# Linear attention of layer 0 in 64-wide blocks, with the small matmuls of a job issued back to back

## The chip, the cores and the metric

One core of one Trainium2 chip runs the whole program. The metric is the device time in microseconds (us) of one execution; the profile is one further execution, recorded by the hardware profiler.

## The reference, cut to what matters

The program is a two-layer trunk (512 tokens, width 1024). Layer 0 mixes tokens with two kinds of linear attention, layer 1 with softmax attention; both have an MLP and a gated side input. The change concerns the second kind of layer 0, with 8 heads of 64 columns:

```python
def rwkv7_scan(r, decay, k, v, kk, a):          # state: [B, H, 64, 64]
    def step(state, inp):
        r_t, w_t, k_t, v_t, kk_t, a_t = inp
        sa = jnp.einsum('bhvk,bhk->bhv', state, -kk_t)
        state = (state * w_t[:, :, None, :] + sa[..., None] * (kk_t * a_t)[:, :, None, :]
                 + v_t[..., None] * k_t[:, :, None, :])
        return state, jnp.einsum('bhvk,bhk->bhv', state, r_t)
```

The kernel does it in chunks of 64 tokens: inside a chunk the recurrence becomes products of 64x64 matrices and one triangular inverse, and a 64x64 state per head goes from chunk to chunk.

## The kernel before, in words

Tiles have 128 partitions, so two heads of 64 columns lie on top of each other: hp = 0 to 3 is a pair of heads, h = 0, 1 the head in it. The 512 tokens are 8 chunks, and g = 0, 1 is a half of four chunks: a = 0, 1 counts pairs of chunks and c_ = 0, 1 the chunk in the pair. One (hp, g) is called a unit here; there are 8 of them. Every matmul of a unit writes a PSUM tile of the ring "pmr", which has four buffers.

- `pre(hp)` makes the vectors of a head pair: bh, kh, the two rows of ar, v.
- `p1(hp, g)` copies bh and kh into BH, a tile in which each head has its own half of the columns and zeros in the other half (L596, ScalarE). The scores come from 8 matmuls of 128 rows and 128 columns (L600); 8 masked products on VectorE (L605) put 64x64 blocks into NA and KA, zeros elsewhere. Eight transposes (L614) are copied to TOK and, with zeros around, to BZ (L617, L619). Four matmuls with KA give TOK's third part (L625), four more the first part of y (L631, copied at L632).
- `p2(hp, g)` inverts four triangular matrices in fp16 (L664 to L684; its first copy is L640) and applies the inverse in four matmuls (L690); the result is MU (L693).
- `p3(hp, g)` makes for each a the state transitions GB and the inputs HS (matmuls L707, L710, L711; L714 on VectorE, L718 on ScalarE), then steps the state (L744, L746), and in `inner` corrects rh_ and y with four matmuls each (L726 and L727, L731 and L732). L754 reads the states.
- `tail(hp)` normalizes and gates the output.

`hgrn` is the other kind of attention (its own PSUM ring "pmh"), the projections are matmuls of 512 columns in three passes (`mm3`, L244 to L246), and `out_piece` adds both results, projected, to x.

Order: every traced instruction has a rank, its place in the program. A scheduler lays out each engine's queue ahead of time: of the instructions that are ready in its own simulation the lowest rank goes first. `tc.high_priority(offset=n)` lowers the ranks inside it by n; `run` does so by 300 for p1, p2, p3 and tail, which `weave` interleaves. On the chip each engine takes its queue strictly in that order. The steps of a head pair follow the string ORDER: A (p2 of half 0 with the p3 of the pair before and p1 of half 1), F (projections), H (hgrn), B, O (out_piece of the pair before), C (p2 of half 1 with the next pre and p3 of half 0, then the next p1).

Of the kernel before, what the change touches and what calls it, by code (L numbers as in the profile page):

```python
# [12 lines left out]
F32 = mybir.dt.float32  # L13
# [21 lines left out]
OFS = 300  # L35
NWARM = 9
# [149 lines left out]
def trunk(ctx, tc, wts, xT, pT, vecs, lora, cst, lev, seg, rope, gain, out, upto="all", dbg=None, mode=None):  # L186
# [97 lines left out]
    class Stats:  # L284
# [4 lines left out]
        def add(self, sq, rhs):  # L289
            for j in range(NJ):  # L290
# [35 lines left out]
    def bcast_rows(rt, cols, pool, tag):  # L326
# [5 lines left out]
        for j in range(NJ):  # L332
# [31 lines left out]
    def layer0_mixer(actp):  # L364
        ph = ExitStack()
        mp = ph.enter_context(tc.tile_pool(name="mp", bufs=1))
        BH = mp.tile([P, 2, 4, P], F32, name="BH")
        NAs = [mp.tile([P, 2, 2, 2, P], F32, name=f"NA{i}") for i in range(2)]
        KAs = mp.tile([P, 2, 2, 2, P], F32, name="KA")
        BZ = [mp.tile([P, 2, 2, 2, P], F32, name=f"BZ{i}") for i in range(2)]  # L370
# [3 lines left out]
        early = [BH, KAs, *NAs, *BZ, GB, SB, PP]  # L374
# [141 lines left out]
        def four(lhs, rhs):  # L516
            ps = pmr.tile([P, S], F32, name="pmr")
            for i in range(4):
# [7 lines left out]
        def pre(hp, r, k, v):  # L526
# [38 lines left out]
            V.tensor_mul(kk, kk, ps)  # L565
            yield
# [9 lines left out]
            V.tensor_mul(bh, bh, pi)  # L576
# [5 lines left out]
            V.tensor_mul(kh, kh, pi)  # L582
            pre_[hp] = (lw, bh, kh, ar, rh_, bo, dl, v, E("y", 2))
# [3 lines left out]

        def p1(hp, g):
            lw, bh, kh, ar, rh_, bo, dl, v, y = pre_[hp]
            gs = slice(g * 256, g * 256 + 256)  # L590
            NA, KA, TOK = NAs[g], KAs, []
            un[hp, g] = (NA, TOK)

            for n, (src, dst) in enumerate(((bh, NA), (kh, KA))):
                for h in range(2):
                    A.copy(BH[hs[h], n, :, hs[h]], src[hs[h], gs].rearrange("p (c t) -> p c t", t=64))  # L596
                ps = pmr.tile([P, S], F32, name="pmr")
                for c_ in range(4):
                    o = g * 256 + c_ * 64
                    T.matmul(ps[:, c_ * P:c_ * P + P].rearrange("p (x t) -> p x t", x=2), BH[:, n, c_, :],  # L600
                             ar[:, :, o:o + 64], start=True, stop=True)
                pv = ps.rearrange("p (a c x t) -> p a c x t", a=2, c=2, x=2)
                for h in range(2):
                    for c_ in range(2):
                        V.tensor_tensor(dst[hs[c_], :, h, :, hs[c_]], pv[hs[h], :, c_, :, :],  # L605
                                        tri[hs[h], None, :, :].to_broadcast([64, 2, 2, 64]), op=OP.mult)
                yield
            for a in range(2):
# [4 lines left out]
                for n, src in enumerate((ar[:, 0, :], v, bh, kh)):  # L613
                    T.transpose(ps[:, n * P:n * P + P], src[:, js], ident)  # L614
# [9 lines left out]
            for i, (a, h) in enumerate(pk):  # L624
                T.matmul(ps[:, i * 64:i * 64 + 64], KA[:, a, h, 0, :], TOK[a][:, 1, hs[h]], start=True, stop=True)  # L625
            for a in range(2):
                A.copy(TOK[a][:, 2, :], ps[:, a * P:a * P + P])
            yield
            ps = pmr.tile([P, S], F32, name="pmr")
            for i, (a, h) in enumerate(pk):  # L630
                T.matmul(ps[hs[h], a * P:a * P + P], TOK[a][:, 1, hs[h]], KA[:, a, h, 1, :], start=True, stop=True)  # L631
            A.copy(y[:, gs], ps[:, :256])  # L632
            yield

        def p2(hp, g):
# [3 lines left out]
            for a in range(2):  # L639
                A.copy(n16[:, 2 * a:2 * a + 2, :], NA[:, a, :, 0, :])  # L640
# [6 lines left out]
            for l in range(1, 6):  # L647
# [12 lines left out]
                def half4(lhs, rhs):  # L660
                    ps = pmr.tile([P, S], F32, name="pmr")
                    pv = ps[:, :256].rearrange("p (i n u) -> p i n u", i=4, u=H)
                    for i in range(4):
# [11 lines left out]
            for i, (a, h) in enumerate(pk):  # L675
                T.matmul(ps[:, i * P:i * P + P], NA[:, a, h, 0, :], tt[:, i, :], start=True, stop=False)
# [5 lines left out]
            for i in range(4):  # L682
# [6 lines left out]
            for i, (a, h) in enumerate(pk):  # L689
                T.matmul(ps[:, i * P:i * P + P].rearrange("p (x f) -> p x f", x=2), tt[:, i, :],  # L690
                         TOK[a][:, 0::2, hs[h]], start=True, stop=True)
            MU = E("MU", 2, [P, 2, 2, P])
            A.copy(MU.rearrange("p a x (h f) -> p a h x f", h=2),  # L693
                   ps.rearrange("p (a h x f) -> p a h x f", a=2, h=2, x=2))
            un[hp, g] = (NA, TOK, MU)
            yield

        def p3(hp, g):
            lw, bh, kh, ar, rh_, bo, dl, v, y = pre_[hp]
            NA, TOK, MU = un.pop((hp, g))  # L700
# [3 lines left out]
            for a in range(2):  # L704
                bz = BZ[g][:, a]
                ps = pmr.tile([P, S], F32, name="pmr")
# [640 lines left out]
```

## Time and profile before

| | us |
|---|---|
| median of 3 runs | 1511.24 (1509.82 to 1512.02) |
| the profiled execution, its own time | 1511.89 |
| its span, first to last instruction | 1510.1 |
| TensorE / VectorE / ScalarE / GpSimd busy | 1478.1 / 937.6 / 663.1 / 138.4 |
| mean granted TensorE clock, share of full speed | 0.997 |

Busy time of TensorE contains the modelled end of each matmul, so a busy engine is not one at its peak. A plain fp32 matmul is recorded as two instructions, an fp32r or fp16 one as a single one.

### The profile page before, as it was taken

How to read it: one execution, taken by the hardware profiler on the slowest of the kernel's cores; microseconds unless marked ns; L12 is line 12 of the kernel's file. 1: busy time of each engine (PE TensorE's matmuls, PEld its weight loads, DVE VectorE, ACT ScalarE, POOL GpSimd, SP SyncE). 2: the span in 40 equal slices, each digit the busy share in tenths (PEclk: the TensorE clock that was granted, in tenths of full speed). 3: DMA queues.
4: the chain of work that ended last, by engine and by line, in shares of the span. 5: the costliest groups of instructions: out<-in, count | busy, mean ns of one | idle time of the engine just before them, and what ended most of it. 6: DMA issues, size and time to landing. Idle time of an engine off the chain costs nothing.

```text
span 1510.1 us, 20495 instructions
## 1 busy us (share of the span) xinstructions
PE 1478.1 (98%) x7546; PEld 1191.3 (79%) x7546; DVE 937.6 (62%) x1835; ACT 663.1 (44%) x1269; POOL 138.4 (9%) x133
## 2 busy tenths in 40 slices
PE   8899999999989999999999999999999999999998
PEld 6678777777667888888888888777778888888887
DVE  6878797687785664444446648377575444445463
ACT  4675545554446433333334534455634333333342
POOL 4121220310205000000000200000220000000000
PEclk9999999999999999999999999999999999999999
DMA  5110111211123233333333432221123333333331
GB/s 179 56 36 22 55 50 39 66 29 47 39 91 106 90 98 98 98 98 98 98 95 98 124 118 84 77 63 50 56 80 95 95 101 98 98 96 93 98 98 70
DMA packets 67109, 123.88 MB, mean 82 GB/s; under 512 B 7632, under 2 KB 8016, under 8 KB 67008
## 3 DMA queue, kind: packets, MB, share of 16 engines
q1 hardware_dynamic: 65376, 118.57, 25.6%
q10 hardware_dynamic: 1152, 2.43, 0.5%
q0 software_dynamic: 480, 1.57, 0.3%
q8 instruction: 59, 0.97, 0.3%
q14 instruction: 42, 0.34, 0.1%
HBM read 120.45 MB, written 2.10 MB: 81 GB/s over the span
## 4 chain that ended last, share of the span: by engine, by line
PE 87%; DVE 7%; ACT 3%; issue 2%; DMA 1%; POOL 1%; SPq 0%; DVEq 0%; ACTq 0%; POOLq 0%
PE pj L244 20%; PE pj L246 20%; PE pj L245 20%; PE pmr L1273 1%; PE pmr L245 1%; PE pmr L1249 1%; PE pmr L246 1%; PE pmr L244 1%; PE pj L1176 1%; PE pmr L1176 1%; PE pj L1178 1%; PE pmr L1177 1%; PE pmr L1178 1%; PE pj L1177 1%; PE pmh L1176 1%
## 5 line engine op out<-in xcount | busy, mean ns | idle before, releaser
L236 ACT CAST whi<-wr 128x512 fp32r<-128x512 f32 x428 | 265.0, 621 | 549.2 <-PE pj L245 421.9
L237 DVE TENSOR_TENSOR wlo<-wr,whi 128x512 fp32r<-128x512 f32 x428 | 312.5, 733 | 197.6 <-ACT whi L236 193.6
L244 PE MATMUL pj<-act,whi 128*128 128x512 f32 (+1 forms) x856 | 338.1, 396 | 1.2 <-DVE h L935 1.0
L245 PE MATMUL pj<-act,whi 128*128 128x512 f32 (+1 forms) x856 | 336.8, 394 | 0.0
L246 PE MATMUL pj<-act,wlo 128*128 128x512 f32 (+1 forms) x856 | 335.7, 393 | 0.5 <-DVE wlo L237 0.5
L244 PE MATMUL pj<-hid,whi 128*128 128x512 f32 x512 | 199.2, 389 | 0.0
L245 PE MATMUL pj<-hid,whi 128*128 128x512 f32 x512 | 199.2, 389 | 0.0
L246 PE MATMUL pj<-hid,wlo 128*128 128x512 f32 x512 | 199.2, 389 | 0.0
L244 PEld LDWEIGHTS pj<-act,whi 128*128 128x128 f32 x856 | 161.1, 188 | 34.4 <-ACT k L491 1.4
L246 PEld LDWEIGHTS pj<-act,wlo 128*128 128x128 f32 x856 | 161.2, 188 | 32.5 <-DVE wlo L237 1.5
L245 PEld LDWEIGHTS pj<-act,whi 128*128 128x128 f32 x856 | 161.2, 188 | 31.1 <-issue 1.5
L1115 DVE TENSOR_TENSOR x<-x,pj 128x512 f32<-128x512 f32 x128 | 88.0, 688 | 80.6 <-PE pj L246 80.2
L245 PEld LDWEIGHTS pj<-hid,whi 128*128 128x128 f32 x512 | 96.1, 188 | 20.0
L244 PEld LDWEIGHTS pj<-hid,whi 128*128 128x128 f32 x512 | 96.1, 188 | 19.9
L246 PEld LDWEIGHTS pj<-hid,wlo 128*128 128x128 f32 x512 | 96.1, 188 | 19.9
L319 POOL TENSOR_TENSOR acc<-acc,xsq 128x512 f32<-128x512 f32 x35 | 48.7, 1393 | 628.8 <-ACT xsq L313 616.0
L1104 DVE SCALAR_TENSOR_TENSOR r<-pj,rb 128x512 f32<-128x512 f32 x56 | 38.7, 691 | 84.0 <-PE pj L246 84.0
L278 DVE TENSOR_TENSOR hid<-r,hid 128x512 fp32r<-128x512 f32 x64 | 44.3, 691 | 41.5 <-ACT hid L277 41.4
L1105 ACT ACTIVATE r<-r 128x512 f32<-128x512 f32 x64 | 40.5, 632 | 21.6 <-DVE r L1104 21.5
L277 ACT CAST hid<-r 128x512 fp32r<-128x512 f32 x64 | 39.8, 621 | 1.9
L280 ACT ACTIVATE act<-x,vec 128x512 fp32r<-128x512 f32 x32 | 22.9, 720 | 29.4 <-DVE x L1133 12.7
L244 PE MATMUL pj<-os,whi 128*128 128x512 f32 x64 | 28.3, 445 | 4.4 <-DVE x L946 2.8
(387 smaller groups left out, 2225.8 us busy)
## 6 DMA issues: line engine op xcount, KB each, us to landing
wr<-in_wts_dram SPq DMA_DIRECT2D x428, 256.0 KB, 2.7
x<-in_xT_dram SPq DMA_DIRECT2D x8, 256.0 KB, 6.3
sr<-in_wts_dram SPq DMA_DIRECT2D x8, 256.0 KB, 5.3
out_dram<-x SPq DMA_DIRECT2D x7, 256.0 KB, 2.0
r<-in_pT_dram ACTq DMA_DIRECT2D x4, 256.0 KB, 3.0
lw<-in_lora_dram POOLq DMA_DIRECT2D x4, 192.0 KB, 3.1
tq<-in_rope_dram ACTq DMA_DIRECT2D x1, 512.0 KB, 6.7
tk<-in_rope_dram ACTq DMA_DIRECT2D x1, 512.0 KB, 7.6
```

Source lines behind the costliest of these rows:

```text
L236: A.copy(hi, raw)
L237: V.tensor_sub(lo, raw, hi.bitcast(F32))
L244: T.matmul(ps, wh, xh, start=first, stop=False)
L245: T.matmul(ps, wh, xl, start=False, stop=False)
L246: T.matmul(ps, wl, xh, start=False, stop=last)
L277: A.copy(h, src)
L278: V.tensor_sub(l, src, h.bitcast(F32))
L319: G.tensor_add(self.t, self.t, sq)
L1104: V.scalar_tensor_tensor(r, q, 0.0, nf[0], op0=OP.max, op1=OP.mult)
L1105: A.activation(r, r, AF.Square)
L1115: V.tensor_add(x[k], x[k], ps)
L1176: T.matmul(ps[j], xh, wh, start=k == 0, stop=False)
```

## The change

The products work on single 64x64 blocks. `bk` holds bh and kh chunk by chunk in one tile, without BH. The scores come from 16 matmuls with 64 rows, 64 stationary columns and 128 moving columns, which take the four quarters of TensorE's array in turn. For the second kind of key the chunk's block lands on the other half of the partitions, so v is copied once per head pair with the two chunks of a pair swapped (`vx`), KA shrinks to the swapped blocks, and the y part that L631 made is gone: it falls out of `inner`, whose stationary operand W now spans both kinds. `p3` makes all transitions and inputs in one job of 16 matmuls with 64 stationary and 64 moving columns, and `inner` is one such job of 16. HS moves from ScalarE to one product on VectorE, and y's addition becomes a copy on ScalarE. `together` and `tight` lower the rank of all matmuls of a job but the first by 40 more; `tight` is put around all loops of small matmuls of layer 0, those of hgrn and the helpers included (`four`, `half4`, `Stats.add`, `bcast_rows`).

```diff
+TIGHT = 40
+    def tight(jobs):
+        for i, job in enumerate(jobs):
+            with tc.high_priority(offset=TIGHT) if i else ExitStack():
+                yield job
...
-        BH = mp.tile([P, 2, 4, P], F32, name="BH")
-        NAs = [mp.tile([P, 2, 2, 2, P], F32, name=f"NA{i}") for i in range(2)]
-        KAs = mp.tile([P, 2, 2, 2, P], F32, name="KA")
-        BZ = [mp.tile([P, 2, 2, 2, P], F32, name=f"BZ{i}") for i in range(2)]
+        NAs = [mp.tile([P, 2, 2, P], F32, name=f"NA{i}") for i in range(2)]
+        KAs = mp.tile([P, 2, 2, P], F32, name="KA")
+        RRs = [mp.tile([P, 2, 2, 2, 64], F32, name=f"RR{i}") for i in range(2)]
+        BKs = [mp.tile([P, 2, 2, P], F32, name=f"BK{i}") for i in range(2)]
+        Ws = [mp.tile([P, 2, 2, 2, P], F32, name=f"W{i}") for i in range(2)]
...
+            vx = E("vx", 1)
+            for c_ in range(2):
+                A.copy(vx.rearrange("p (j c t) -> p j c t", c=2, t=64)[:, :, 1 - c_],
+                       v.rearrange("p (j c t) -> p j c t", c=2, t=64)[:, :, c_])
...
-            V.tensor_mul(bh, bh, pi)
+            V.tensor_mul(bk[:, :, 0::3, :], jc(bh), jc(pi))
...
-            V.tensor_mul(kh, kh, pi)
+            V.tensor_mul(bk[:, :, 1:3, :], jc(kh), jc(pi))
...
+        def together(jobs):
+            for i, (out, lhs, rhs) in enumerate(jobs):
+                with tc.high_priority(offset=TIGHT) if i else ExitStack():
+                    T.matmul(out, lhs, rhs, start=True, stop=True)
...
-            for n, (src, dst) in enumerate(((bh, NA), (kh, KA))):
-                for h in range(2):
-                    A.copy(BH[hs[h], n, :, hs[h]], src[hs[h], gs].rearrange("p (c t) -> p c t", t=64))
-                ps = pmr.tile([P, S], F32, name="pmr")
-                for c_ in range(4):
-                    o = g * 256 + c_ * 64
-                    T.matmul(ps[:, c_ * P:c_ * P + P].rearrange("p (x t) -> p x t", x=2), BH[:, n, c_, :],
-                             ar[:, :, o:o + 64], start=True, stop=True)
-                pv = ps.rearrange("p (a c x t) -> p a c x t", a=2, c=2, x=2)
-                for h in range(2):
-                    for c_ in range(2):
-                        V.tensor_tensor(dst[hs[c_], :, h, :, hs[c_]], pv[hs[h], :, c_, :, :],
-                                        tri[hs[h], None, :, :].to_broadcast([64, 2, 2, 64]), op=OP.mult)
-                yield
+            pq = [pmr.tile([P, S], F32, name="pmr").rearrange("p (c a x t) -> p c a x t", c=2, a=2, x=2)
+                  for h in range(2)]
+            for a in tight(range(2)):
+                for c_ in range(2):
+                    o = g * 256 + a * P + c_ * 64
+                    for n in range(2):
+                        at = bk[:, 2 * g + a, 3 * c_ if n == 0 else 1 + c_, :]
+                        for h in range(2):
+                            T.matmul(pq[h][hs[c_ ^ n], c_, a], at[hs[h]], ar[hs[h], :, o:o + 64],
+                                     start=True, stop=True)
+            yield
+            for h in range(2):
+                for r in range(2):
+                    V.tensor_tensor(NA[hs[r], :, h, hs[r]], pq[h][hs[r], r, :, 0, :],
+                                    tri[hs[r], 0:1, :].to_broadcast([64, 2, 64]), op=OP.mult)
+                V.tensor_tensor(RR[:, :, h].rearrange("p a c t -> p c a t"), pq[h][:, :, :, 1, :],
+                                tri[:, 1:2, None, :].to_broadcast([P, 2, 2, 64]), op=OP.mult)
+                for r in range(2):
+                    V.tensor_tensor(KA[hs[r], :, h, hs[1 - r]], pq[h][hs[r], 1 - r, :, 0, :],
+                                    tri[hs[r], 0:1, :].to_broadcast([64, 2, 64]), op=OP.mult)
+            yield
...
+                A.copy(BKs[g][:, a], pv[:, 2:4, :])
                 for c_ in range(2):
-                    A.copy(BZ[g][hs[c_], a, :, c_, :], pv[hs[c_], 2:4, :])
+                    A.copy(W_[hs[1 - c_], a, c_, 1, :], pv[hs[1 - c_], 1, :])
...
-            for i, (a, h) in enumerate(pk):
-                T.matmul(ps[hs[h], a * P:a * P + P], TOK[a][:, 1, hs[h]], KA[:, a, h, 1, :], start=True, stop=True)
-            A.copy(y[:, gs], ps[:, :256])
...
-            for a in range(2):
-                A.copy(n16[:, 2 * a:2 * a + 2, :], NA[:, a, :, 0, :])
+            A.copy(n16, NA.rearrange("p a h t -> p (a h) t"))
...
-            A.copy(MU.rearrange("p a x (h f) -> p a h x f", h=2),
-                   ps.rearrange("p (a h x f) -> p a h x f", a=2, h=2, x=2))
+            for c_ in range(2):
+                A.copy(Ws[g][hs[c_], :, c_].rearrange("p a x (h f) -> p a h x f", h=2), pv[hs[c_]])
...
-            for a in range(2):
-                bz = BZ[g][:, a]
-                ps = pmr.tile([P, S], F32, name="pmr")
-                T.matmul(ps[:, :256], MU[:, a, 0, :], bz[:, 0].rearrange("p c f -> p (c f)"), start=True, stop=True)
-                for c_ in range(2):
-                    o = ps[:, 256 + c_ * P:256 + c_ * P + P]
-                    T.matmul(o, bz[:, 0, c_, :], MU[:, a, 1, :], start=True, stop=False)
-                    T.matmul(o, bz[:, 1, c_, :], TOK[a][:, 1, :], start=False, stop=True)
...
+            for k in range(4):
+                a, c_ = divmod(k, 2)
+                w, b = W_[:, a, c_], BKs[g][:, a, c_]
+                jobs += [(pv[hs[h], k, 0], w[:, 0, hs[h]], b[:, hs[h]]) for h in range(2)]
+                jobs += [(pv[hs[h], k, 1], b[:, hs[h]], w[:, 1, hs[h]]) for h in range(2)]
+            together(jobs)
+            yield
+            for h in range(2):
+                V.tensor_tensor(GB[hs[h], :, hs[h]], pv[hs[h], :, 0, :],
+                                cc("istack")[hs[h], None, :].to_broadcast([64, 4, 64]), op=OP.add)
+            V.tensor_tensor(HS, pv[:, :, 1, :], dl[:, 4 * g:4 * g + 4, None].to_broadcast([P, 4, 64]), op=OP.mult)
...
-                for i, (a, h) in enumerate(pk):
-                    T.matmul(ps[hs[h], a * P:a * P + P], MU[:, a, 1, hs[h]], NA[:, a, h, 1, :], start=True, stop=True)
-                V.tensor_add(y[:, gs], y[:, gs], ps[:, :256])
+                together([(pv[hs[h], x_, 2 * a + c_], W_[:, a, c_, x_, hs[h]], RR[:, a, h, c_, :])
+                          for x_ in range(2) for a in range(2) for c_ in range(2) for h in range(2)])
+                yield
                 V.tensor_add(rh_[:, gs], rh_[:, gs], ps[:, :256])
+                A.copy(y[:, gs], ps[:, 256:])
```

## Rows read from the trace of the kernel before

**Rows 1.** Page, part 1: busy time, share of the span, instructions.

```profile
PE 1478.1 (98%) x7546; PEld 1191.3 (79%) x7546; DVE 937.6 (62%) x1835; ACT 663.1 (44%) x1269; POOL 138.4 (9%) x133
```

**Rows 2.** Windows of the span: length, busy time of each engine, clock, DMA.

```profile
60.00:160.00 100.00, 96.65 (x786) 77.58 (x785) 79.66 (x199) 61.02 (x148) 18.33 (x20) 1.00 0.12 34
160.00:262.00 102.00, 99.05 (x683) 78.38 (x682) 82.47 (x190) 55.98 (x123) 20.40 (x20) 1.00 0.15 45
262.00:366.00 104.00, 101.75 (x695) 80.02 (x693) 79.80 (x188) 54.47 (x121) 18.18 (x17) 1.00 0.16 47
...
396.00:453.00 57.00, 50.03 (x284) 39.07 (x284) 47.14 (x106) 25.28 (x53) 9.17 (x8) 0.97 0.23 70
453.00:1510.00 1057.00, 1048.45 (x4700) 855.39 (x4698) 588.49 (x1027) 422.42 (x748) 48.74 (x35) 1.00 0.30 92
```

**Rows 3.** TensorE's waits, 60 to 440 us: total, times, longest.

```profile
PE pj L244 <- DVE x L946: 2.5, 3, 1.3
PE pj L244 <- ACT os L277: 1.7, 1, 1.7
```

**Rows 4.** The chain that ended last, 223 to 229 us: start, length.

```profile
223.93 1.80 PE pmr L600 x16
```

**Rows 5.** TensorE's timeline, 407 to 416 us: start, length, instruction.

```profile
407.70 0.44 PE L690 MATMUL pmr<-TOK,tt 128*128 128x128 f32 x2
...
409.68 0.66 PE L690 MATMUL pmr<-TOK,tt 128*128 128x128 f32 x4
...
411.01 0.70 PE L707 MATMUL pmr<-BZ,MU 128*128 128x256 f32 x2 [0.35 <-ACT MU L693]
...
413.85 0.49 PE L744 MATMUL pmr<-SB,GB 128*128 128x128 f32 x2
414.26 0.66 PE L726 MATMUL pmr<-NA,MU 128*64 128x128 f32 x8
414.85 0.71 PE L873 MATMUL pmh<-vt,h 128*128 128x128 f32 x4
```

**Rows 6.** Groups of TensorE, 60 to 453 us: count, busy, mean ns.

```profile
L600 PE MATMUL pmr<-ar,BH 128*128 128x128 f32 x128 | 17.6, 282 | 1.0 <-issue 1.0
...
L631 PE MATMUL pmr<-KA,TOK 128*64 128x128 f32 x64 | 7.6, 291 | 0.0
L731 PE MATMUL pmr<-NA,MU 128*64 128x128 f32 x64 | 6.3, 287 | 0.0
```

**Rows 7.** TensorE's timeline, 210 to 225 us, the reads of the states.

```profile
216.30 0.86 PE L754 MATMUL pmr<-ar,SB 128*128 128x64 f32 x6
216.97 0.48 PE L244 MATMUL pj<-os,whi 128*128 128x512 f32 x1
```

**Rows 8.** TensorE's timeline, 381 to 385 us, two kinds in turn.

```profile
381.05 0.39 PE L245 MATMUL pj<-act,whi 128*128 128x512 f32 x1
381.28 0.40 PE L246 MATMUL pj<-act,wlo 128*128 128x512 f32 x1
381.61 0.43 PE L731 MATMUL pmr<-NA,MU 128*64 128x128 f32 x2
381.97 0.50 PE L244 MATMUL pj<-act,whi 128*128 128x512 f32 x1
382.40 0.43 PE L731 MATMUL pmr<-NA,MU 128*64 128x128 f32 x2
```

**Rows 9.** Groups of VectorE and ScalarE, 60 to 453 us.

```profile
L605 DVE TENSOR_TENSOR NA<-pmr,cs 64x256 f32<-64x256 f32 x32 | 13.5, 420 | 1.9 <-PE pmr L600 1.5
L714 DVE TENSOR_TENSOR GB<-pmr,cs 64x128 f32<-64x128 f32 x32 | 9.2, 288 | 21.5 <-PE pmr L711 18.6 <-ACT HS L718 2.4
L732 DVE TENSOR_TENSOR y<-y,pmr 128x256 f32<-128x256 f32 x8 | 3.4, 419 | 3.0 <-PE pmr L731 2.9
...
L718 ACT ACTIVATE HS<-pmr,dl 64x64 f32<-64x64 f32 x64 | 16.4, 303 | 18.0 <-DVE GB L714 17.1
L596 ACT COPY BH<-bh 64x256 f32<-64x256 f32 x16 | 6.4, 402 | 8.4 <-PE pmr L600 4.3 <-DVE bh L576 4.0
L693 ACT COPY MU<-pmr 128x512 f32<-128x512 f32 x8 | 4.7, 584 | 6.8 <-PE pmr L690 6.8
```

More of the change, by code (lines that the diff above doesn't have):

```diff
@@ L289, in add @@
         def add(self, sq, rhs):
-            for j in range(NJ):
+            for j in tight(range(NJ)):
                 T.matmul(self.ps[:, j * self.cols:(j + 1) * self.cols], sq[:, j * P:(j + 1) * P], rhs,
@@ L331, in bcast_rows @@
                           rt[:, :, None].to_broadcast([P, NJ * cols, P // cols]))
-        for j in range(NJ):
+        for j in tight(range(NJ)):
             lhs = full[:, j * P:(j + 1) * P] if cols > 1 else rt[:, j:j + 1].to_broadcast([P, P])
@@ L517, in four @@
             ps = pmr.tile([P, S], F32, name="pmr")
-            for i in range(4):
+            for i in tight(range(4)):
                 T.matmul(ps[:, i * P:i * P + P], lhs(i), rhs(i), start=True, stop=True)
@@ L662, in half4 @@
                     pv = ps[:, :256].rearrange("p (i n u) -> p i n u", i=4, u=H)
-                    for i in range(4):
+                    for i in tight(range(4)):
                         T.matmul(pv[:, i], lhs[:, i, :], rhs[:, i], start=True, stop=True)
@@ L674, in p2 @@
             ps = pmr.tile([P, S], F32, name="pmr")
-            for i, (a, h) in enumerate(pk):
-                T.matmul(ps[:, i * P:i * P + P], NA[:, a, h, 0, :], tt[:, i, :], start=True, stop=False)
+            for i, (a, h) in tight(enumerate(pk)):
+                T.matmul(ps[:, i * P:i * P + P], NA[:, a, h, :], tt[:, i, :], start=True, stop=False)
                 T.matmul(ps[:, i * P:i * P + P], id16, id16, start=False, stop=True)
@@ L681, in p2 @@
             ps = pmr.tile([P, S], F32, name="pmr")
-            for i in range(4):
+            for i in tight(range(4)):
                 T.matmul(ps[:, i * P:i * P + P], er[:, i, :], XT[:, i, :], start=True, stop=False)
@@ new lines, in p3 @@
+            pv = ps.rearrange("p (k x f) -> p k x f", k=4, x=2)
+            jobs = []
+            for k in range(4):
[8 more added lines that the diff above has]
+                                cc("istack")[hs[h], None, :].to_broadcast([64, 4, 64]), op=OP.add)
@@ L751, in p3 @@
             f = 1 if g == 0 else 0
-            for c_ in range(f, 4):
+            for c_ in tight(range(f, 4)):
                 ch = 4 * g + c_
@@ L759, in tail @@
         def tail(hp):
[L760 removed]
+            lw, bk, ar, rh_, bo, dl, vx, y = pre_.pop(hp)
             dump(f"y{hp}", y)
@@ L801, in hgrn @@
             ps = pmh.tile([P, S], F32, name="pmh")
-            for j in range(NJ):
+            for j in tight(range(NJ)):
                 T.transpose(ps[:, j * P:j * P + P], iv[:, j * P:j * P + P], ident)
@@ L828, in hgrn @@
             ps = pmh.tile([P, S], F32, name="pmh")
-            for j in range(NJ):
+            for j in tight(range(NJ)):
                 js = slice(j * P, j * P + P)
@@ L848, in hgrn @@
                 ps = pmh.tile([P, S], F32, name="pmh")
-                for j in range(NJ):
+                for j in tight(range(NJ)):
                     js = slice(j * P, j * P + P)
@@ L866, in hgrn @@
             ps = pmh.tile([P, S], F32, name="pmh")
-            for j in range(3):
+            for j in tight(range(3)):
                 T.transpose(ps[:, j * P:j * P + P], d[:, j * P:j * P + P], ident)
@@ L871, in hgrn @@
             ps = pmh.tile([P, S], F32, name="pmh")
-            for j in range(3):
+            for j in tight(range(3)):
                 T.matmul(ps[:, j * P:j * P + P], kt[:, j * P:j * P + P], vt[:, j, :], start=True, stop=True)
@@ L879, in hgrn @@
             ps = pmh.tile([P, S], F32, name="pmh")
-            for j in range(NJ):
+            for j in tight(range(NJ)):
                 js = slice(j * P, j * P + P)
@@ L894, in hgrn @@
             ps = pmh.tile([P, S], F32, name="pmh")
-            for j in range(NJ):
+            for j in tight(range(NJ)):
                 T.transpose(ps[:, j * P:j * P + P], ot[:, j * P:j * P + P], ident)
```

51 lines of the change are left out of this document (22 added, 29 removed).

## The prediction

> **What bounds the kernel now.** I read the page first: TensorE is busy 98% of the span, the next engine, VectorE, 62% [rows 1]. Then the windows by stage. The linear attentions and their projections lie between 60 and 396 us; in the three whole stretches shown TensorE is busy 97% (297.5 of 306 us) and VectorE 79% (241.9 us) [rows 2]. From 396 to 453 us, where the last head pair finishes and its output is projected, TensorE falls to 88% and the clock to 0.97. Behind 453 us the change moves nothing but a few transposes' ranks. So TensorE's work between 60 and 396 us sets the pace, and time saved there should be seen at the end; the waits of TensorE from 60 to 440 us are small, the largest two being for x (L946) and for the split output (L277), 2.5 and 1.7 us in total [rows 3], both in the last stretch.
>
> **TensorE's work, unit by unit** (8 units, one per hp and g; all by start to next start, since busy time holds the modelled ends).
>
> Removed. The scores (L600) are 16 recorded instructions in 1.80 us [rows 4], 0.112 each. The transitions and inputs (L707, L710, L711) run from 411.01 to 413.85: 2.84 us. The corrections (L726) run from 414.26 to 414.85: 0.59 us for 8 instructions [rows 5]; L731 and L631 have the same shape and count [rows 6], so three such jobs make 1.77 us. Together 1.80 + 2.84 + 1.77 = 6.41 us.
>
> Slots. The 8 instructions of L726 have 64 stationary columns and alternate between the two column halves. At 0.112 us each one after another they would take 0.90 us; they take 0.59. So two run at once: 4 slots of 0.112 are 0.45, and 0.14 is left for entering and leaving. The six instructions of L754, 128 stationary but only 64 moving columns, take 0.67 us from 216.30 to 216.97 [rows 7], again 0.112 each. Halving the moving side alone buys nothing; there the load of 128 stationary columns is the limit, and it hides the moving side. With 64 stationary and 64 moving columns both are halved; my estimate is 0.056 us for a slot of two.
>
> Added. p3's job and inner's job are each 32 recorded instructions, 16 slots of two. Bounds: 0.056 us a slot (both sides halved) and 0.112 (nothing gained from the shorter side). I take 0.056, since L754 against L600 shows load and stream overlapped. That is 16 x 0.056 + 0.14 = 1.04 us each, at the upper bound 1.93. The scores are 32 instructions with 128 moving columns over four quarters of the array. The trace shows two column halves at once, but no two row halves. Bounds: 8 slots of four (8 x 0.112 + 0.14 = 1.04 us), or every instruction alone (32 x 0.112 + 0.14 = 3.72); between them lie 16 slots of two, as L726 does it (1.93). I take 1.04: the nearest row, L726, shows that matmuls on separate parts of the array don't wait for each other.
>
> Sum per unit: 3 x 1.04 = 3.12 in place of 6.41, 3.3 us less, 26 us for eight. With row halves in sequence 4.01, 19 us for eight; with narrow slots at 0.112 as well 5.79, 5 us; with every score alone too 7.58, 9 us more than before.
>
> **What changing the shape costs.** At 381 us L731 alternates with 512-column matmuls. One round, from 381.61 to 382.40, takes 0.79 us; the large matmul accounts for 0.23 (L245 to L246) and two instructions for 0.22, so going in and out of the narrow shape costs 0.34 us, and the pair is not overlapped [rows 8]. In rows 5 it is the same: L726 starts 0.41 us after L744 where 0.22 would do, 0.19 more, and 0.14 lies inside. There are three narrow jobs per unit before (L631, L726, L731) and three after, so this cancels as long as each job stays whole. The Trainium skill speaks against the change at this point: TensorEngine Tiling (Array Packing), Key Properties, says that changing the tiling mode drains TensorE, and that tiles work independently. By that rule each job split by other work pays again; the 0.34 us of the trace agree with the drain, and the sum above would stay for whole jobs.
>
> **The ranks.** They matter for that reason: L731's job at 381 us is broken three times, 3 x 0.34 = 1.0 us. In L690's job at the end the first two instructions start at 407.70 and the last four at 409.68, ending at 410.34 [rows 5]; whole, it takes 8 x 0.112 plus a tail of 0.2, so MU's data would be there 1.5 us earlier. But it then needs two ScalarE copies of 512 columns instead of one, 0.58 us more [rows 9], and hgrn's matmuls stand behind. I book 1.0 us for the breaks and 0.5 for the end; bounds 0 and 3.
>
> **The other engines.** VectorE, per unit: eight products of L605 at 0.42, four of L714 at 0.29 and two additions at 0.42 [rows 9] make 5.4 us. After: eight products of half the size (0.29, by L714's shape), two for RR, two for GB, one for HS and one addition at 0.42 make 4.8. ScalarE loses four copies of L596 at 0.40 and eight of L718 at 0.30, and pays about one more long copy and some short ones: some 3 us less per unit. Neither is on the path by itself; TensorE covers both, and if that cover went, the changes would still be gains. NA is complete after seven products instead of four, about 1 us later, at p1's end; the next p2 waits for it through its first copy, and behind that the fp16 matmuls, but projections fill TensorE meanwhile. GpSimd (9% busy, rows 1) only writes fewer zeros at the start. No DMA is added or moved.
>
> **What arrives at the end.** Not all of 26 us: the chain of a unit through VectorE and ScalarE keeps its steps, VectorE would be busy in over 80% of the shorter stretch, and the last unit falls into the stretch with 88%. Between all of it (TensorE 97% busy) and a quarter I take two thirds, 17.6 us. With 1.0 and 0.5: 19.1 us. The profiled execution took 1511.9 us, 1.8 above its span and 0.65 above the median of 1511.2. So 1511.9 - 19.1 = 1492.8 for it, and 1492 as the median.
>
> **Rivals.**
> - *Narrow matmuls don't get shorter slots.* Place: p3 and inner, 0.112 us a slot. With the scores at 1.04 a unit takes 4.90 and 12 us are saved, two thirds of it 8; with scores in slots of two, 5 and 3. Time 1502 to 1507. For it: no row has both sides narrow. Against it: the load hides the stream in L754. The Trainium skill, TensorE: Matmul & The Clock Gate, "What overlaps and what doesn't", lets a load overlap a running matmul only where the row group differs, which would bring this case; L754's 0.112 speaks against it here.
> - *The saved time becomes waiting.* VectorE or the unit's own chain sets the pace once TensorE is lighter; a quarter of 26 us arrives, 6.6: time 1504. For it: VectorE 79%. Against it: TensorE's waits are under 3% now. It decides when VectorE passes 90% over 60 to 396 us.
> - *Slower: quarters one at a time.* If the scores' quarters take turns and the narrow slots stay at 0.112, a unit costs 7.58: 9 us more, 1520. With narrow slots at 0.112 the sign turns where a job of scores costs over 2.55 us (6.41 - 2 x 1.93); with narrow slots at 0.056 even scores one at a time (3.72) stay below it (4.33). For it: no row of before has row halves at once.
> - *Nothing moves.* The two errors meet in the middle, for instance slots of two with 0.112 and a third of 5 us: 1509 to 1512.
>
> **How the numbers follow.** Forecast 0.60 (1483 to 1500: all of 26 us plus 2, or half of it), first rival 0.12, second 0.12, slower 0.10, no change 0.06. The measurement can tell about 0.2%, 3 us, from nothing. Faster takes the first three, less what of them lies above 1508: 0.83. Same 0.07, slower 0.10. The range reaches from 1482 to 1507 and leaves out the slower case and no change.
>
> **What would show it.** In the new trace a whole score job should take about 1.0 us from start to next start, p3's and inner's jobs 1.0 us each; four starts a few ns apart in the scores say that row halves run together. The stretch from the first score to the last output projection should be about 19 us shorter, TensorE's idle share there not above 5%, VectorE's busy share 80 to 85%. The prediction is wrong if the narrow jobs last 2 us or more, if they lie in pieces between 512-column matmuls, or if TensorE's idle time grows by what its work shrank.

## The result, and the profile after

The changed kernel takes 1494.76 us (median of four runs, 1491.57 to 1496.35) beside 1511.63 for the kernel before: a ratio of 0.9884, 95% interval 0.9872 to 0.9897. The forecast was 1492.0, in a range from 1482 to 1507. The profiled execution took 1493.68 us, its span is 1491.9, and TensorE's mean granted clock in it 0.994 (0.997 before).

Busy time of the whole span, as in [rows 1]:

```profile
PE 1452.8 (97%) x7834; PEld 1176.4 (79%) x7834; DVE 932.8 (63%) x1835; ACT 642.5 (43%) x1197; POOL 138.9 (9%) x132
```

TensorE lost 25 us of busy time. The windows, cut so that the last two answer to the last two of [rows 2] (columns as there: length, busy time of TensorE, its loads, VectorE, ScalarE and GpSimd, clock, DMA):

```profile
60.00:155.00 95.00, 88.37 (x852) 71.01 (x851) 75.59 (x193) 52.98 (x124) 18.55 (x19) 0.98 0.12 34
155.00:251.00 96.00, 91.61 (x757) 72.96 (x756) 81.06 (x196) 48.09 (x101) 21.18 (x20) 1.00 0.13 44
251.00:348.00 97.00, 93.38 (x759) 75.17 (x757) 77.56 (x186) 49.09 (x102) 19.02 (x18) 1.00 0.16 51
348.00:380.00 32.00, 31.98 (x331) 24.63 (x329) 20.39 (x51) 12.01 (x24) 0.62 (x1) 1.00 0.18 59
380.00:436.50 56.50, 46.33 (x219) 35.78 (x219) 46.41 (x96) 27.07 (x48) 10.78 (x9) 0.94 0.24 75
436.50:1491.90 1055.40, 1046.71 (x4700) 854.43 (x4698) 588.48 (x1027) 422.47 (x748) 48.67 (x35) 1.00 0.29 92
```

The attentions took 336 us (60 to 396) and now take 320 (60 to 380). The stretch behind them, up to the last output projection, is as long as it was, 56.5 us beside 57.0. What comes after that took 1057 us and takes 1055.4, with 3.4 us at the lower clock in place of 6.8. So nearly all of the gain, 16 us, lies ahead of 380 us. There TensorE was idle for 14.7 of 320 us (4.6%) and VectorE busy for 254.6 (79.6%). Over the stretch that the prediction named, from the first score to the last output projection, the windows of before and after are:

```profile
64.26:452.47 388.21, 373.07 (x2608) 292.92 (x2608) 301.50 (x713) 207.19 (x464) 66.44 (x64) 1.00 0.16 48
62.94:436.04 373.10, 348.27 (x2899) 277.34 (x2899) 298.00 (x713) 187.53 (x394) 67.86 (x64) 0.99 0.16 49
```

TensorE is idle for 24.8 us of it, 6.7%, beside 15.1 us (3.9%) before.

TensorE's timeline at the first scores, and at p3's and inner's jobs of the last unit (start, length, instruction; a row of x32 is a whole job):

```profile
62.94 1.38 PE L626 MATMUL pmr<-ar,bk 64*64 64x128 f32 x32
64.25 0.33 PE L644 MATMUL pmr<-cs,ar 128*128 128x128 f32 x1
...
372.21 0.34 PE L610 MATMUL pmr<-BK,W 128*64 128x64 f32 x4
...
373.48 0.50 PE L253 MATMUL pj<-act,wlo 128*128 128x512 f32 x1
...
375.05 1.15 PE L610 MATMUL pmr<-RR,W 128*64 128x64 f32 x32
376.13 0.50 PE L252 MATMUL pj<-act,whi 128*128 128x512 f32 x1
376.47 0.38 PE L769 MATMUL pmr<-SB,GB 128*128 128x128 f32 x2
376.61 0.47 PE L253 MATMUL pj<-act,wlo 128*128 128x512 f32 x1
376.92 0.39 PE L251 MATMUL pj<-act,whi 128*128 128x512 f32 x1
```

From start to next start the scores take 1.31 us, p3's job 1.27 here, where its second and third group of four start 0.26 us apart, and inner's 1.08, which is what 11 of the 16 narrow jobs take. L626 and L610 stand in the place of L600, L631 and L731 of [rows 6] and of L707 to L711 and L726 of [rows 5].

TensorE's waits from 60 to 424 us (total, times, longest; [rows 3] are those of before):

```profile
PE pmr L705 <- ACT tt L702: 3.5, 5, 1.3
PE pmr L693 <- DVE X L698: 3.5, 5, 1.6
PE pj L251 <- DVE x L971: 3.3, 4, 1.2
PE pmh L876 <- DVE KS L872: 2.7, 1, 2.7
PE pj L251 <- ACT os L284: 2.0, 1, 2.0
...
PE pmr L693 <- ACT PP L696: 0.9, 2, 0.7
```

The triangular inverse (L693, L705) waits inside its own chain for 7.9 us in these rows. Before the change, from 60 to 440 us, its waits (L664, L690) were 4.8:

```profile
PE pmr L664 <- ACT PP L667: 1.5, 2, 0.7
...
PE pmr L664 <- ACT BZ L619: 1.1, 2, 0.5
PE pmr L690 <- ACT tt L685: 1.1, 3, 0.7
PE pmr L664 <- DVE X L669: 1.1, 3, 0.4
```

And hgrn's last block (L876) now waits alone. What follows such a wait is in the timeline and in two windows at hgrn's last block:

```profile
396.62 3.65 PE L876 MATMUL pmh<-qs,KS 128*128 128x64 f32 x16 [2.69 <-DVE KS L872]
...
400.59 0.63 PE L252 MATMUL pj<-os,whi 128*128 128x512 f32 x1
401.02 0.63 PE L253 MATMUL pj<-os,wlo 128*128 128x512 f32 x1
```

```profile
392.00:396.00 4.00, 1.92 (x14) 1.47 (x13) 4.00 (x7) 1.44 (x4) 3.58 (x3) 0.97 0.18 64
396.00:400.00 4.00, 3.38 (x16) 3.42 (x17) 3.46 (x6) 2.23 (x6) 2.41 (x4) 0.50 0.01 2
```

The granted clock is 0.50, the lower of the two levels (1.2 GHz), and the 512-column matmuls L252 and L253 start 0.43 us apart instead of 0.23. Until the last output projection the clock is at that level for 13.7 us (from 57.8, 112.4 and 395.8 us on, each time in or right behind a wait of TensorE of 1.7 to 2.7 us), beside 3.4 us before the change. Not every such wait is followed by it: a second profile of the changed kernel ("changed, again" below) has the waits at 58 and 111 us too, 1.9 and 1.7 us long, and the clock stays at 1.00 there.

**Where the time went.** For each kernel I divide the time up to the start of its last output projection of layer 0 into three: TensorE's idle time; half of the time in which it worked at 1.2 GHz, since a large matmul takes 0.43 us there and 0.23 at full speed, nearly twice as long; and the rest, work at full speed. For the kernel before this is 452.5 = 23.4 + 1.7 + 427.4, for the changed one 436.0 = 30.4 + 6.4 + 399.2. Work fell by 28.2 us; 7.0 came back as waits and 4.7 as low clock; 16.5 arrived. The second profile of the changed kernel gives 29.6, 8.0, 3.1 and 18.6.

### The profile page after: what moved, and what is told of

Same layout as the page of the kernel before. It is cut to its first block, busy times and chain, and to the rows that moved or that the text cites. A ratio compares the mean times of both kernels' runs of the same rounds, so it can differ in the third digit from the quotient of the medians.

```text
span 1491.9 us, 21002 instructions
## 1 busy us (share of the span) xinstructions
PE 1452.8 (97%) x7834; PEld 1176.4 (79%) x7834; DVE 932.8 (63%) x1835; ACT 642.5 (43%) x1197; POOL 138.9 (9%) x132
## 4 chain that ended last, share of the span: by engine, by line
PE 68%; DVE 2%; ACT 1%; POOL 0%; issue 0%; DVEq 0%; ACTq 0%; POOLq 0%
PE pj L251 18%; PE pj L252 17%; PE pj L253 17%; PE pmr L1298 1%; PE pmr L1274 1%; PE pj L1201 1%; PE pmr L1201 1%; PE pj L1203 1%; PE pmr L1203 1%; PE pmr L1202 1%; PE pj L1202 1%; PE pmh L1201 1%; PE pmh L1203 1%; PE pmh L1202 1%; PE pmr L252 1%; PE pmr L251 1%
## 5 line engine op out<-in xcount | busy, mean ns | idle before, releaser
L252 PE MATMUL pj<-act,whi 128*128 128x512 f32 (+1 forms) x856 | 337.7, 396 | 0.0
L253 PE MATMUL pj<-act,wlo 128*128 128x512 f32 (+1 forms) x856 | 336.3, 394 | 1.1 <-DVE wlo L238 1.1
L253 PE MATMUL pj<-hid,wlo 128*128 128x512 f32 x512 | 199.4, 389 | 0.0
L252 PE MATMUL pj<-hid,whi 128*128 128x512 f32 x512 | 199.4, 389 | 0.0
L253 PEld LDWEIGHTS pj<-act,wlo 128*128 128x128 f32 x856 | 161.4, 189 | 35.3 <-DVE wlo L238 2.2
L252 PEld LDWEIGHTS pj<-act,whi 128*128 128x128 f32 x856 | 161.6, 189 | 32.4 <-issue 2.0
L253 PEld LDWEIGHTS pj<-hid,wlo 128*128 128x128 f32 x512 | 96.1, 188 | 20.0
L252 PEld LDWEIGHTS pj<-hid,whi 128*128 128x128 f32 x512 | 96.1, 188 | 19.8
L288 DVE SCALAR_TENSOR_TENSOR act<-x,vec,act 128x512 fp32r<-128x512 f32 x32 | 28.4, 893 | 10.2 <-ACT act L287 10.2
```

## Experiments

All kernels but one (before with ranks alone) start from the changed kernel. Ratios are to the kernel before, in runs on the same chip; four chips were used, on which its median was 1510.4 to 1512.2 us, so small differences are better read from the ratios than from the medians. "Granted clock" is the median over the runs of each kernel (for the kernel before, over its 56 runs beside the experiments); "idle", "clock" and "work" are the three parts just described, from the one profile of each kernel. How far they depend on the execution can be seen from the two profiles of the changed kernel.

| kernel | us, median (range) | ratio [95%] | granted clock | last projection at | idle | clock | work |
|---|---|---|---|---|---|---|---|
| before | 1511.63 | 1 | 0.997 | 452.5 | 23.4 | 1.7 | 427.4 |
| changed | 1494.76 (1491.57–1496.35) | 0.9884 [0.9872, 0.9897] | 0.9935 | 436.0 | 30.4 | 6.4 | 399.2 |
| changed, again | 1495.39 (1491.65–1502.85) | 0.9894 [0.9874, 0.9913] | 0.9935 | 433.9 | 31.4 | 4.8 | 397.8 |
| blocks alone | 1500.92 (1495.24–1501.75) | 0.9929 [0.9913, 0.9946] | 0.993 | 440.3 | 23.4 | 5.1 | 411.8 |
| ranks alone | 1515.49 (1514.82–1518.56) | 1.0035 [1.0022, 1.0048] | 0.9935 | 460.8 | 30.5 | 11.6 | 418.7 |
| ranks on narrow jobs | 1498.76 (1491.66–1501.13) | 0.9908 [0.9887, 0.9928] | 0.991 | 432.9 | 27.4 | 3.4 | 402.1 |
| scores by quarter | 1500.29 (1498.62–1505.99) | 0.9928 [0.991, 0.9945] | 0.993 | 446.8 | 29.4 | 9.7 | 407.7 |
| halves not in turn | 1508.09 (1503.58–1511.74) | 0.9976 [0.9963, 0.9989] | 0.992 | 449.3 | 28.7 | 9.9 | 410.7 |
| scores twice | 1515.14 (1510.31–1517.63) | 1.0025 [1.0014, 1.0036] | 0.9915 | 457.0 | 32.6 | 8.5 | 415.9 |
| scores in order | 1494.37 (1492.1–1499.19) | 0.9894 [0.9878, 0.9911] | 0.9935 | 439.8 | 32.7 | 10.6 | 396.5 |
| narrow jobs whole | 1498.74 (1496.66–1503.34) | 0.9918 [0.99, 0.9936] | 0.9905 | 442.6 | 32.1 | 11.7 | 398.8 |
| F and H of h=3 early | 1500.19 (1497.58–1501.95) | 0.9928 [0.9916, 0.994] | 0.9905 | 439.7 | 34.1 | 8.2 | 397.4 |
| F of h=3 early | 1495.26 (1490.85–1496.52) | 0.9887 [0.9871, 0.9904] | 0.993 | 435.5 | 29.3 | 6.8 | 399.4 |
| hgrn filled | 1495.7 (1494.76–1497.07) | 0.9894 [0.9879, 0.9908] | 0.9945 | 435.8 | 29.4 | 3.4 | 403.0 |

### Which part of the change does it

**Blocks alone**: no rank is lowered.

```diff
-            with tc.high_priority(offset=TIGHT) if i else ExitStack():
-                yield job
+            yield job
...
-                with tc.high_priority(offset=TIGHT) if i else ExitStack():
-                    T.matmul(out, lhs, rhs, start=True, stop=True)
+                T.matmul(out, lhs, rhs, start=True, stop=True)
```

> The 64x64 blocks without the lowered ranks. Theory (ranks are booked at 1.5 us, the blocks carry the rest): 1496 us, between 1494 and 1499. Rival (the ranks are what keeps the narrow jobs whole; without them a job falls into pieces and each change of shape costs 0.34 us): 1501 to 1508, with the pieces to be seen in the timeline of the score, transition and correction jobs.

6 us slower than the changed kernel, so the rival was nearer. The 16 narrow jobs (L608 here) lie in 49 pieces between other matmuls, in 20 in the changed kernel. TensorE's timeline of this kernel shows one of them:

```profile
95.43 0.49 PE L250 MATMUL pj<-act,whi 128*128 128x512 f32 x1
95.86 0.33 PE L608 MATMUL pmr<-W,BK 128*64 128x64 f32 x2
96.11 0.50 PE L251 MATMUL pj<-act,whi 128*128 128x512 f32 x1
96.55 0.33 PE L608 MATMUL pmr<-BK,W 128*64 128x64 f32 x2
```

One round takes 0.69 us; 0.23 is the large matmul, 0.12 the two instructions, and 0.34 remains: the price of [rows 8] again. It belongs to the change of shape: a job of full width, broken in the same way, pays nothing, since in the changed kernel's timeline above two instructions of L769 and one large matmul take 0.45 us from 376.47 to 376.92, which is 0.22 and 0.23. 29 more breaks by 0.34 are 9.9 us of the 12.6 by which this kernel's work exceeds the changed one's. But the ranks gave only half of that to the end: idle time is 23.4 us without them, 30.4 with them. Of these 7 us 5 lie behind 380 us (5.0 idle without the ranks, 10.2 with them). Without them the last unit's p3 runs there, in turn with hgrn's last block (L874), as before the change:

```profile
397.80 1.74 PE L874 MATMUL pmh<-qs,KS 128*128 128x64 f32 x8 [0.61 <-DVE KS L870]
...
403.73 0.48 PE L608 MATMUL pmr<-BK,W 128*64 128x64 f32 x4
```

With them that unit's p3 runs from 372 to 379 us, and hgrn's last block has only the tail and projections beside it while it waits for its own chain.

**Ranks alone**: the kernel before, with the same lowered ranks at its own jobs.

```diff
-            for i in range(4):
+            for i in tight(range(4)):
...
-            for i, (a, h) in enumerate(pk):
+            for i, (a, h) in tight(enumerate(pk)):
...
```

> The kernel before with the lowered ranks alone. Theory: 1.5 us less than before, 1510, within what the measurement can tell from nothing. Rival (the ranks order more than the narrow jobs, those of hgrn and of the inverse too, and bring a share of the 17 us by themselves): 1501 to 1507.

Missed: the ranks alone make the old kernel 5 us slower. Work fell by 8.7 us, as whole jobs should make it; idle time rose by 7.1, the same as from blocks alone to the changed kernel, and the clock was low for 13.7 us without a break, from 417.5 us on, as the windows show. In the runs its median is 0.9935 beside 0.997; at 0.8 to 1.7 us for each 0.001 (last section) that is 3 to 6 us, so the lower clock alone can be the 5 us.

```profile
420.00:424.00 4.00, 4.00 (x17) 3.52 (x15) 1.84 (x5) 0.00 (x0) 0.59 (x1) 0.50 0.00 0
424.00:428.00 4.00, 3.43 (x16) 3.03 (x16) 2.43 (x5) 0.48 (x1) 0.00 (x0) 0.50 0.22 72
```

**Ranks on narrow jobs only**, with the plain loops as they were:

```diff
     def tight(jobs):
         for i, job in enumerate(jobs):
-            with tc.high_priority(offset=TIGHT) if i else ExitStack():
-                yield job
+            yield job
...
-            for a in tight(range(2)):
-                for c_ in range(2):
+            for a in range(2):
+                with tc.high_priority(offset=TIGHT) if a else ExitStack():
+                  for c_ in range(2):
```

> The changed kernel with the lowered ranks on the narrow jobs alone (scores, transitions, corrections), all other small loops in plain order. Theory (the ranks pay by keeping narrow jobs whole, 29 breaks of 0.34 us fewer than without; on the other loops they only bring waits, since alone they made the old kernel 5 us slower): no slower than the changed kernel, 1489 to 1495. Rival (the ranks of the fp16 and hgrn loops bring their share): 1497 to 1501.

Its median is 4 us above the changed kernel's, but its six runs spread from 1491.66 (mean clock 0.997) to 1501.13 (0.989). The median lies in the rival's range, but whether the plain loops' ranks are worth anything stays open: the intervals overlap. Its profile, of a run of 1492.05 us, has the last unit's p3 at 389.5 us, beside hgrn's last block again, less idle time than the changed kernel (27.4 us) and the earliest end of all (432.9).

### Does the array run as forecast

**Scores by quarter**: all matmuls of one quarter in a row.

```diff
-            for a in tight(range(2)):
-                for c_ in range(2):
...
+            for h in tight(range(2)):
+                for r in range(2):
+                    for a in range(2):
+                        for c_ in range(2):
...
```

> The changed kernel with the same 16 score matmuls sorted by quarter of the array: four in one quarter, then four in the next. Theory (four quarters run at once, 0.112 us a slot): a score job grows from about 1.05 to about 3.6 us, 2.5 us in each of 8 units, 20 us of TensorE time, of which two thirds or more arrive: 1508 to 1515. Rival (quarters take turns anyway, or only two run at once): 0 to 8 us more, 1495 to 1503.

The edit is not clean: the lowered ranks of the second half let it overtake the first, so that two quarters run mixed. The job takes 2.29 us (timeline below) and not 3.6. Where two neighbours share a quarter they start 109 ns apart, elsewhere 6 to 7 ns. About 1 us more per unit made 5.5 us in time. The time lies in the rival's range, but not for the rival's reason: quarters do run at once, and the edit broke up less of that than was meant.

```profile
65.01 2.35 PE L626 MATMUL pmr<-ar,bk 64*64 64x128 f32 x32
67.30 0.33 PE L644 MATMUL pmr<-cs,ar 128*128 128x128 f32 x1
```

**Halves not in turn**: p3's and inner's matmuls sorted so that one column half comes first and then the other.

```diff
-            together(jobs)
+            together(jobs[0::2] + jobs[1::2])
...
-                          for x_ in range(2) for a in range(2) for c_ in range(2) for h in range(2)])
+                          for h in range(2) for x_ in range(2) for a in range(2) for c_ in range(2)])
```

> The changed kernel with the 16 matmuls of the transition job and of the correction job sorted by head, so that the column half changes once per job and not after every matmul. Theory (two column halves run at once; both sides narrow make a slot of 0.058 us, so one alone takes that too): a job grows from 1.08 to about 1.9 us, 0.8 us in each of 16 jobs, 13 us of TensorE time, 1504 to 1510. Rival (loading the next block is what a slot waits for, and loads of one half can't run under its own matmul): 0.11 us each, 3.5 us a job, 1520 and more.

As expected: 13.3 us more, in the theory's range. The timeline shows inner's job 1.84 us to the next start, 0.057 for each of 32 records:

```profile
107.96 1.90 PE L610 MATMUL pmr<-RR,W 128*64 128x64 f32 x32
109.80 0.29 PE L693 MATMUL pmr<-PP,XT 128*128 128x64 f16 x4
```

So the slot of 64 by 64 columns is half of 0.112 by itself, and the two column halves then run at once (pairs start 6 to 7 ns apart, the next pair 52 ns later). The Trainium skill, TensorE: Matmul & The Clock Gate, "What overlaps and what doesn't", lets a load overlap a running matmul only where the row groups differ. All these matmuls use all 128 rows, and load and stream still overlap, since each load is recorded with 0.14 us and the next one starts 0.058 us later: the trace disagrees.

**Scores twice**: each score matmul is issued twice into the same place.

```diff
-            for a in tight(range(2)):
+            for a in tight([0, 1, 0, 1]):
```

> The changed kernel with the scores computed twice, the second time over the first. It adds 8 x 0.96 us of TensorE time and nothing to the other engines, but makes the scores' products start 1 us later. Theory (TensorE sets the pace between 60 and 380 us, two thirds or more arrive): 5 to 8 us more, 1500 to 1503. Rival (TensorE time has become cheap, the waits take it up): 0 to 2 us more, 1495 to 1497.

Missed, and this says most about the step with "two thirds": a score job takes 3.05 us in the timeline, 1.74 more, 14 us for eight units, and the kernel became 20 us slower, two or three of which go with a lower clock (0.9915). TensorE time added to this stretch arrives in full.

```profile
65.20 3.12 PE L626 MATMUL pmr<-ar,bk 64*64 64x128 f32 x64 [0.25 <-DVE bk L594]
68.25 0.33 PE L644 MATMUL pmr<-cs,ar 128*128 128x128 f32 x1
```

**Scores in order**: the ranks of all score matmuls but the first are lowered, instead of those of the second half.

```diff
+            jobs = []
+            for a in range(2):
...
+                        jobs += [(pq[h][hs[c_ ^ n], c_, a], at[hs[h]], ar[hs[h], :, o:o + 64]) for h in range(2)]
+            together(jobs)
```

> The changed kernel with the lowered rank on all score matmuls but the very first, in place of on the second half of them. In the changed kernel the second half overtakes the first and the quarters no longer come in turn, a job takes 1.31 us; without ranks it took 1.03. Theory: 1.03 us again, 0.3 us in each of 8 jobs, 2 us less, 1492 to 1494. Rival (the order inside the job is hidden): no change, 1494 to 1496.

The whole job (L610 here, since it goes through `together`) takes 1.04 us, as forecast for the quarters:

```profile
62.17 1.10 PE L610 MATMUL pmr<-ar,bk 64*64 64x128 f32 x32 [0.25 <-DVE bk L594]
63.21 0.33 PE L644 MATMUL pmr<-cs,ar 128*128 128x128 f32 x1
```

In blocks alone four starts lie within 20 ns and the next four follow 109 ns after; in the changed kernel the second half overtakes the first, the quarters are out of turn, and the job takes 1.31. But the median did not move (1494.37, in the rival's range). Work fell by 2.7 us; this profile has more low clock (10.6 us lost).

**Narrow jobs whole**: scores in order and lowered ranks on the narrow jobs alone.

> The changed kernel with the lowered ranks on all three kinds of narrow jobs but their first matmul, scores too, and plain order in all other small loops. Theory (only whole narrow jobs pay): as the changed kernel at an equal clock, some 1486 at full clock, and 1491 to 1497 in time, more or less by what the clock does: 1.3 to 1.5 us for each 0.001 of the mean clock. Rival (the ranks on the fp16 and hgrn loops save TensorE time of their own): 1498 and more, slower also at an equal clock.

Slower than the changed kernel, 1498.74 at mean clocks of 0.990 to 0.993, with intervals that do not overlap. The theory's range is missed; the rival's is met in time, but TensorE's work is that of the changed kernel (398.8). What its profile has more of is low clock (11.7 us lost) and idle time (32.1).

### Where the rest went

**F and H of h=3 early**: the last hgrn block and its projections rank 300 lower.

```diff
-                step(c, h)
+                with tc.high_priority(offset=OFS) if h == 3 and c in "FH" else ExitStack():
+                    step(c, h)
```

> The changed kernel with the projections and hgrn of the last head pair raised by 300 ranks too, so that they run beside the last units and not after them. Theory (the last 56 us, from 380 us on, did not get shorter because hgrn's chain is alone there and TensorE is busy 82% of it): the stretch from the end of the last unit shrinks, 3 to 8 us less, 1487 to 1492. Rival (the work has the same sum and the waits move to another place): within 2 us of 1495, or more if the units are held up.

My theory was that hgrn's last block ends late because it ranks low. It failed: 5 us slower, of which the lower clock (0.9905 beside 0.9935) can be 2 to 5; TensorE's work did not rise. The order was only turned round, as the timeline shows: hgrn ran first and p3 of the last unit came last.

```profile
386.43 1.06 PE L907 MATMUL pmh<-vt,at 128*128 128x128 f32 x4
...
408.19 0.34 PE L610 MATMUL pmr<-BK,W 128*64 128x64 f32 x4
```

**F of h=3 early**: the same for the projections alone (`c == "F"`).

> The changed kernel with only the three projections of the last head pair's hgrn raised by 300 ranks, hgrn itself left at its rank. Theory (in the kernel with both raised, hgrn ran whole before the last inverse and the two chains stood one behind the other; with the projections alone early, hgrn's operands are there while the last inverse runs, and the two chains overlap): the stretch from 348 us on shrinks, 1487 to 1492. Rival (the projections are the filler that the last inverse needs; taken early, TensorE waits there): 1495 to 1500.

No change (1495.26). TensorE's waits from 340 to 440 us fell from 10.2 to 6.9 us and the end came no earlier.

**hgrn filled**: ten more 64-column matmuls ahead of the four of the last two levels in hgrn's last block, to shorten the wait that precedes the low clock. The four overwrite what the ten wrote.

```diff
+                if h == 3 and l in (3, 4):
+                    for _ in range(10):
+                        T.matmul(ps[:, :64], KS[1 - l % 2][:, :P], q_[:, :64], start=True, stop=True)
+                q_ = qs
```

> The changed kernel, with 10 more 64-column matmuls into the same PSUM tile ahead of the four score matmuls of the last two levels of the intra-chunk attention of layer 0's last block (h=3, l=3 and 4); the four that follow overwrite what they wrote, so that the result is the same. They need only data that is there already and shorten TensorE's two waits there (1.3 us for h and 2.7 us for KS before 396.6 us). Theory (the low clock behind a wait is part of what the change gives back): the granted clock between 391 and 407 us stays at or near 1.00 instead of 6.8 us at 0.5, so 3 to 4 us come back, mean clock 0.996, median 1490.5 to 1492.5. Rival (the clock's fall is set by something else than this wait, or the end is held by VectorE and ScalarE alone): clock there as before, or the time unchanged in spite of it, 1494 to 1497.

Run beside it on the same chip, the changed kernel once more:

> The changed kernel itself, for comparison with the version with the added matmuls on the same chip. Both theories: 1494 to 1496 us, mean clock 0.993 to 0.995, about 6.8 us at half clock between 391 and 407 us.

Half of the theory held. In the changed kernel's second profile the timeline and the windows show the wait of 2.69 us and the low clock behind it again:

```profile
394.29 3.65 PE L876 MATMUL pmh<-qs,KS 128*128 128x64 f32 x16 [2.69 <-DVE KS L872]
```

```profile
392.00:396.00 4.00, 1.72 (x8) 1.75 (x9) 4.00 (x6) 2.03 (x6) 3.15 (x4) 0.71 0.19 66
396.00:400.00 4.00, 4.00 (x16) 3.52 (x16) 3.06 (x8) 1.29 (x3) 2.12 (x2) 0.50 0.00 0
```

With the added matmuls (L876 here; the four are L880) the two waits for KS are 0.38 and 0.69 us, and the clock stays at 1.00:

```profile
393.11 2.40 PE L876 MATMUL pmh<-qs,KS 128*128 128x64 f32 x20
395.31 0.47 PE L253 MATMUL pj<-os,wlo 128*128 128x512 f32 x1
396.16 1.10 PE L880 MATMUL pmh<-qs,KS 128*128 128x64 f32 x8 [0.38 <-DVE KS L872]
```

```profile
392.00:396.00 4.00, 3.79 (x31) 3.34 (x29) 4.00 (x6) 1.58 (x5) 3.78 (x3) 1.00 0.22 69
396.00:400.00 4.00, 3.84 (x34) 3.84 (x35) 2.98 (x6) 2.46 (x6) 2.58 (x3) 1.00 0.00 1
```

The time did not move (1495.7 beside 1495.39). The filling itself takes 2.2 us at each of its two places, 4.4 together, and the 6.8 us of low clock cost at most 3.4. So that the wait brings the low clock is supported at this place; that the end would come earlier without it is not shown.

## Why the prediction was right, by its own steps

- **Slots of the narrow jobs, 1.04 us a job: right.** 11 of the 16 jobs take 1.08 us, one 1.27, and four, broken once, 1.23 us in their two pieces. Halves not in turn shows both factors, the slot of 0.057 and two at once. The first rival falls.
- **Scores, 1.04 us: right for the array, mis-sized for the kernel.** In turn the quarters take 1.03 to 1.04; in the changed kernel five jobs take 1.31 and three, broken once, 1.66. The slower rival falls: four quarters run at once.
- **Sum per unit: 3.12 forecast, 3.70 measured** (1.44 for the scores, 2.26 for two narrow jobs). From 6.41 that is 2.7 less and 21.7 for eight, where 26 were forecast.
- **Changing the shape cancels: right.** Before, L631, L726 and L731 lie in 34 pieces between other matmuls; after, all 24 narrow jobs, scores included, lie in 31.
- **Ranks, 1.5 us: mis-sized, and with two signs.** 28.2 - 21.7 = 6.5 us of TensorE's work is left over for them and the new order; this is a remainder that no run isolates, but on the old kernel they took 8.7 us off the work by themselves. In time, on the blocks they gave 6 us, because blocks alone break into 49 pieces at 0.34 us each; on the old kernel they cost 5, much or all of it by the lower clock. I priced one broken job of the old kernel and not what the scheduler does with jobs of 32 instructions. Nor did I price the waits: idle time is 7 us higher with ranks in both pairs of kernels. TensorEngine Tiling (Array Packing), Key Properties, of the Trainium skill (a change of the tiling mode drains TensorE) agrees with the 0.34 us, which the trace gives and the page does not.
- **What arrives, two thirds of 26 plus 1.5 = 19.1: the sum near, its reason half right.** TensorE's work fell by 28.2 us, ranks included, and 16.5 arrived, 0.59 of it. I put the loss down to VectorE and the unit's chain. VectorE was not the bound by its busy share, 79.9% between the first score and the last projection, and the second rival's sign (90%) did not come. The unit's chain is there: the inverse's waits rose from 4.8 to 7.9 us. But the rest of the 7.0 us of waits is mainly hgrn's last block, left alone at the end (L856, L876 and L898 wait 4.6 us behind 380 us, where it was 1.7), and 4.7 us are low clock; neither stood in the sum. As a total the waits came with the ranks: blocks alone has no more idle time than the kernel before, 12.2 us of its 15.6 arrived and 3.4 went to the clock.
- **The last stretch: it gives nothing, but not through the last unit.** It took 57.0 us and takes 56.5; before [rows 2] TensorE was idle there for 7.0 us, now for 10.2. The prediction had the last unit in it. That unit's p3 ran at 411 us [rows 5] and now runs at 372, ahead of it, where TensorE is busy for 31.98 of 32 us. Which of its chains sets the end stays open: hgrn's last block and the last head pair each came last in one kernel or another, and no reordering shortened both.
- **Idle share not above 5%: missed.** Between the first score and the last output projection it is 6.7%; the 4.6% hold only up to 380 us. **VectorE 80 to 85%: at the lower edge** (79.9%). **Stretch 19 us shorter: 15.1.** **Idle time not growing by what the work shrank: right,** 9.7 us more on this stretch.

The forecast of 1492 lies 2.8 us below the median. In TensorE's work two errors in size nearly cancel, 4.3 us too much for the blocks and 5.0 too little for the ranks; that much of the nearness is luck. What is left is the share that arrives: 19.1 of 27.5 us forecast, 16.5 of 28.2 measured, and the low clock, which I had not counted, is larger than that difference.

## What to carry to other kernels

Price a saving on the engine that sets the pace in full, and then look for what it uncovers: here 28 us of TensorE's work became 16.5 us of time, and the rest turned into waits and into a lower clock behind waits. Small matmuls of another shape than their neighbours gain from being kept whole, at 0.34 us per break, but the same ranks brought 7 us of waits here, 5 of them where they had moved work away from beside a slow chain: run them without the edit that they were meant for, and look at the idle time. Look at the granted clock of both kernels' runs before calling a few microseconds a gain or a loss.

## What the runs showed of the hardware

- Matmuls on the four quarters of the array, taken in turn (blocks alone), start 6 to 7 ns apart; the next on the same quarter starts 109 ns after, with 64 stationary and 128 moving columns in fp32. With 128 rows, 64 stationary and 64 moving columns the other column half starts 6 to 7 ns later and the same half again after 58 ns.
- Going from 512-column matmuls of full width into a job of 64 stationary columns and back costs 0.34 us (0.79 - 0.23 - 0.22 before, 0.69 - 0.23 - 0.12 in blocks alone); into a job of full width and back, nothing (0.45 - 0.23 - 0.22 in the changed kernel).
- The spread of one kernel's runs follows the granted clock: ten runs of the changed kernel go from 1502.85 us at a mean of 0.990 to 1491.57 and 1493.20 at 0.996, 1.7 us for each 0.001 by a straight line; 0.001 of 1492 us is 1.5 us. The same line through 56 runs of the kernel before, at 0.993 to 0.998, gives only 0.8. The median of the clock over these 56 runs is 0.997, over the ten 0.9935. The difference is worth 3 to 6 us by these rates; the profiles have 4.7 and 3.1.
